# Both norms after the output projection from sums gathered per product, with all products ahead of the norms

## The chip, the cores and the metric

One core of one Trainium2 chip runs the whole program in one launch. The metric is the device time of an execution in microseconds; less is better. Engines are named as in the profile: PE is TensorE's matmul, DVE is VectorE, ACT is ScalarE, POOL is GpSimd, SP is SyncE, which issues the weight loads.

## What is computed

Two layers of one trunk over 512 latent tokens and 256 context tokens, 1024 features wide. What matters here is what stands around the output projection `w_out` of each layer, where a norm of its result `y` is added to the residual `x`, and a norm of the new `x` feeds the feed-forward part:

```python
def rmsnorm(x, g):
    y = xf * lax.rsqrt(jnp.mean(xf * xf, axis=-1, keepdims=True) + NORM_EPS)
    return y.astype(x.dtype) * g
...
    y_x = merge_heads(...) @ w_out
...
        x = x + mod_x[2] * rmsnorm(y_x, norm_mix_post[i])
        hx = modulate(rmsnorm(x, norm_ffn_pre[i]), mod_x[3], mod_x[4])
        x = x + mod_x[5] * rmsnorm(conv_ffn(hx, ...), norm_ffn_post[i])
        if not last:
            xc = xc + mod_c[2] * rmsnorm(y_c, norm_mix_post[i])
            hc = modulate(rmsnorm(xc, norm_ffn_pre[i]), mod_c[3], mod_c[4])
```

In the last layer only the latent tokens are carried on.

## The kernel before

Activations lie features first: eight tiles of 128 features by 768 tokens, columns 0 to 255 the context (`CS`), 256 to 767 the latent tokens (`XS`). Every product is made of three: `wsplit` loads 128 x 1024 weights and splits each half into a rounded `wh` (ACT, line 191) and a rest `wl` (DVE, line 192); `fsteps` then issues 24 matmuls for a tile of 128 outputs, over 8 feature tiles, of `wl` and `wh` against the activation's `hh`, `hl` (or `mh`, `ml` for the mixed heads). A product accumulates in one of **two** PSUM buffers `bb`, and the next but one can start only when ACT or DVE has read it.

The output projection (lines 375 to 395 of `layer`) runs segment by segment: `XS` then `CS` in layer 0, the two halves of `XS` in layer 1. Each segment has eight products, each copied by ACT to `y` (line 385), and then two norms. `post` makes the first: `rms` of `y` (ACT squares, line 503; sums over the tiles on DVE and POOL by turns, line 505; a sum over the partitions by matmuls with `ones`; a root and a reciprocal, lines 243 and 244; a broadcast over the partitions by matmuls, `cst,rms`; ACT copies the result to `rb`, line 521), then `y` times gate times `rb` (DVE, line 531) and `x += y` (DVE and POOL by turns, line 532). `prenorm` makes the second in the same way, from squares of the new `x`; per tile it leaves `v` (lines 543 and 547), `hh` (544, 548) and `hl` (545 on DVE, 549 and 550 with POOL), which the feed-forward products read.

Tiles come from pools with a tag and a number of buffers: squares and `v` share the tag `sq` with three buffers, sums take `acc` with four. The order of every engine's instructions is not that of the source: a scheduler, asked for by `TCK=dict(schedule_with_timeline_sim=True)`, arranges them by a timeline of its own. So products of the next part may stand ahead of norms of this one, and a change in one place can move rows in others. The same `post` and `prenorm` close the feed-forward part (`tail`), and there layer 0 hands over to layer 1: the last segment, the context, is normed while the first products of layer 1's input projection run, which ACT copies out of `bb` to `u` (line 822 of before, line 885 of the change).

Of the kernel before, what the change touches and what calls it, by code (L numbers as in the profile page):

```python
# [19 lines left out]
D = 1024  # L20
KT = 8
# [9 lines left out]
XS, CS = (256, 768), (0, 256)  # L31
# [7 lines left out]
SQB = 3  # L39
# [15 lines left out]
SQ0, MG, PR = 0, 0, 0  # L55
ACB, RBB = 4, 2
WB, RB = 3, 2
# [78 lines left out]
class Net:  # L136
# [124 lines left out]
    def main(self):  # L261
        nc, tc, a = self.nc, self.tc, self.a
# [23 lines left out]
        Np, N = self.pool("N")  # L286
# [7 lines left out]
        self.load_params(0)  # L294
        rbs = [self.rms(N, self.xt, *s, True) for s in (XS, CS)]
        self.tick(99)
# [14 lines left out]
    def layer(self, l, later):  # L311
        nc, tc, a = self.nc, self.tc, self.a
# [86 lines left out]
        g = self.gate(1)  # L399
# [89 lines left out]

    def rms(self, N, src, a, b, copy=False):  # L490

# [18 lines left out]
        for t in range(nt):  # L510
            for i, z in enumerate(acc):
                self.mm(ps[:, t:t + 1], z[:, t * 128:(t + 1) * 128], self.ones[:, 0:1], i == 0, i == len(acc) - 1)
        r = self.small(4, "rms", 4)[:, :nt]
        self.rsqrt(r, ps[:, :nt], 1.0 / D, self.eps[:, 0:1])
        ps = self.ab()
        for t in range(nt):
            self.mm(ps[:, t * 128:(t + 1) * 128], r[:, t:t + 1].to_broadcast([128, 128]), self.c("ident"), True, True)
# [4 lines left out]
        return rb  # L522

    def post(self, N, s, seg, y, g=None):
# [9 lines left out]
    def prenorm(self, N, s, seg, rb=None):  # L534

        nc, (a, b) = self.nc, seg
        sc, sh = self.coefs(s, 1 if a < 256 else 0)
        rb = self.rms(N, self.xt, a, b) if rb is None else rb
        for k in range(KT):
# [1026 lines left out]
```

## Time and profile before

| | us |
|---|---|
| median of three runs | 2274.95 (2271.13 to 2276.51) |
| the profiled execution, own time | 2278.35 |
| its span, first to last instruction | 2276.6 |
| PE busy, share of the span | 2045.0, 90% |
| DVE busy | 1310.4, 58% |
| ACT busy | 1008.7, 44% |
| POOL busy | 536.0, 24% |

Busy means that an instruction of the engine was running. PE is the engine to watch; its idle stretches, and stretches in which its granted clock is under 1.00 of full speed, are where time can be won or lost. Layer 0's output projection lies at 653 to 778 us of the span with its norms, the handover to layer 1 at 1346 to 1400 us, and layer 1's output projection at 1836 to 1932 us.

### The profile page before, as it was taken

The numbers are of one execution on the slowest core, as the hardware profiler recorded it, in microseconds if no ns is written. First come the engines' busy times: TensorE is split into PE (matmuls) and PEld (weight loads), VectorE is DVE, ScalarE is ACT, GpSimd is POOL, SyncE is SP. The second block draws the span as 40 slices with busy tenths as digits, with TensorE's granted clock in tenths as the row PEclk, the third lists the DMA queues.
The fourth block names the chain that finished last, engine by engine and source line by source line (L and its number), as shares of the span: only waits on it lengthen the run. The fifth ranks groups of instructions, "written<-read, shape, count | busy, mean of one in ns | idle before, by whom it ended". The sixth has DMA issues, their size and how long they took to land. (4 is left out here: it accounts for less than half of the span.)

```text
span 2276.6 us, 44601 instructions
## 1 busy us (share of the span) xinstructions
PE 2045.0 (90%) x18168; PEld 1672.8 (73%) x18168; DVE 1310.4 (58%) x2474; ACT 1008.7 (44%) x1928; POOL 536.0 (24%) x897
## 2 busy tenths in 40 slices
PE   7898999888888799999999969988988777999996
PEld 4677777765667578888888857876766567888886
DVE  3354535668845743354454686556667757655556
ACT  4553323565464633332232456633446446543333
POOL 1342121135502310000010143413122613211102
PEclk8799999998898999999999979999989988999997
DMA  6232345422042354422212333111412053323322
GB/s 262 67 118 100 109 148 164 143 66 68 13 149 92 121 179 167 157 103 65 66 57 66 102 109 124 61 44 62 155 43 96 6 171 102 111 94 96 99 94 92
DMA packets 85134, 235.64 MB, mean 104 GB/s; under 512 B 9088, under 2 KB 24896, under 8 KB 84928
## 3 DMA queue, kind: packets, MB, share of 16 engines
q1 hardware_dynamic: 84928, 232.78, 30.7%
q8 instruction: 143, 2.34, 0.4%
q14 instruction: 63, 0.52, 0.1%
HBM read 204.04 MB, written 28.70 MB: 102 GB/s over the span
## 5 line engine op out<-in xcount | busy, mean ns | idle before, releaser
L212 PE MATMUL bb<-hh,wl 128*128 128x512 f32 (+1 forms) x1520 | 548.3, 361 | 18.0 <-DVE wl L192 10.9
L212 PE MATMUL bb<-hl,wh 128*128 128x512 f32 (+1 forms) x1520 | 542.0, 357 | 5.8 <-POOL hl L550 4.4
L192 DVE TENSOR_TENSOR wl<-wr,wh 128x512 fp32r<-128x512 f32 (+2 forms) x452 | 338.3, 751 | 362.3 <-ACT wh L191 361.0
L212 PE MATMUL bb<-hh,wh 128*128 128x512 f32 (+1 forms) x1520 | 540.2, 355 | 0.0
L191 ACT CAST wh<-wr 128x512 fp32r<-128x512 f32 (+2 forms) x452 | 274.1, 611 | 518.0 <-PE bb L212 370.3
L212 PEld LDWEIGHTS bb<-hh,wl 128*128 128x128 f32 x1520 | 293.2, 193 | 75.2 <-DVE wl L192 14.0
L212 PEld LDWEIGHTS bb<-hl,wh 128*128 128x128 f32 x1520 | 292.8, 193 | 49.4 <-POOL hl L550 7.8
L212 PEld LDWEIGHTS bb<-hh,wh 128*128 128x128 f32 x1520 | 292.9, 193 | 39.6 <-issue 2.1
L212 PE MATMUL bb<-g,wh 128*128 128x512 f32 (+1 forms) x1024 | 263.7, 349 | 2.3 <-DVE g L192 2.3
L1441 POOL TENSOR_SCALAR y<-u,fmt 128x512 f32<-128x512 f32 (+2 forms) x88 | 80.6, 917 | 527.1 <-ACT u L824 525.6
L212 PEld LDWEIGHTS bb<-g,wh 128*128 128x128 f32 x1024 | 181.5, 195 | 27.5 <-DVE g L192 3.3
L212 PE MATMUL bb<-g,wl 128*128 128x512 f32 (+1 forms) x512 | 180.3, 354 | 21.4 <-DVE wl L192 8.5
L212 PEld LDWEIGHTS bb<-g,wl 128*128 128x128 f32 x512 | 99.2, 195 | 36.9 <-ACT g L191 9.3
L824 ACT ACTIVATE u<-bb,fmt 128x512 f32<-128x512 f32 (+1 forms) x118 | 69.0, 613 | 85.0 <-PE bb L212 85.0
L212 PE MATMUL bb<-mh,wl 128*128 128x256 f32 (+1 forms) x256 | 85.2, 333 | 23.4 <-DVE wl L192 15.5
L1468 DVE TENSOR_TENSOR y<-y,bb 128x512 f32<-128x512 f32 (+2 forms) x80 | 54.8, 686 | 82.3 <-PE bb L212 82.2
L505 POOL TENSOR_TENSOR acc<-acc,sq 128x256 f32<-128x256 f32 (+1 forms) x48 | 49.5, 1031 | 183.9 <-ACT sq L503 180.9
L1442 DVE SCALAR_TENSOR_TENSOR y<-u,fmt,y 128x512 f32<-128x512 f32 (+2 forms) x88 | 72.3, 822 | 29.6 <-POOL y L1441 29.6
L212 PE MATMUL bb<-ml,wh 128*128 128x256 f32 (+1 forms) x256 | 84.1, 329 | 0.3
L1380 ACT ACTIVATE P<-bb,ast,srq 128x768 f32<-128x768 f32 (+1 forms) x80 | 72.6, 908 | 23.4 <-DVE ast L1378 14.5
L212 PE MATMUL bb<-mh,wh 128*128 128x256 f32 (+1 forms) x256 | 82.9, 324 | 0.0
L1377 DVE TENSOR_REDUCE ast<-bb 128x1 f32<-128x768 f32 (+1 forms) x80 | 67.2, 842 | 15.9 <-PE bb L212 15.6
(519 smaller groups left out, 3680.4 us busy)
## 6 DMA issues: line engine op xcount, KB each, us to landing
wr<-in_ffn_w_in SPq DMA_DIRECT2D x92, 512.0 KB, 3.5
wr<-in_w_ada SPq DMA_DIRECT2D x80, 512.0 KB, 3.9
wr<-in_ffn_w_out SPq DMA_DIRECT2D x48, 512.0 KB, 3.5
wr<-in_w_in SPq DMA_DIRECT2D x40, 512.0 KB, 4.3
wr<-in_w_out SPq DMA_DIRECT2D x32, 512.0 KB, 3.5
aw<-in_w_ada SPq DMA_DIRECT2D x16, 512.0 KB, 8.5
x<-in_xT SPq DMA_DIRECT2D x16, 384.0 KB, 8.7
wr<-in_w_uq SPq DMA_DIRECT2D x16, 192.0 KB, 2.6
```

The costliest lines, as they stand in the source:

```text
L191: self.nc.scalar.copy(hi, src)
L192: (eng or self.nc.vector).tensor_tensor(lo, src, hi.bitcast(F32), op=ALU.subtract)
L212: self.nc.tensor.matmul(out, l, r, start=start, stop=stop)
L505: (nc.vector, nc.gpsimd)[k % 2].tensor_tensor(acc[k % 2], acc[k % 2], sq, op=ALU.add)
L824: nc.scalar.activation(u[:, a + o:b + o], ps[:, off + a:off + b], AF.Identity, bias=bias)
L1377: nc.vector.reduce_max(st[:, 0:1], sc, axis=AX)
L1380: nc.scalar.activation(P[:, :w], sc, AF.Exp, bias=st[:, 0:1], scale=self.srq[:, t:t + 1], accum_out=st[:, 1:2])
L1441: nc.gpsimd.tensor_scalar(yv, u[:, lo + 1:lo + 1 + n], cw[1], self.fm(P_FCB + i), op0=ALU.mult, op1=ALU.add)
L1442: nc.vector.scalar_tensor_tensor(yv, u[:, lo:lo + n], cw[0], yv, op0=ALU.mult, op1=ALU.add)
L1468: nc.vector.tensor_tensor(y, y, p, op=ALU.add)
```

## The change

For each product tile the new `sums` takes, from `y` as it comes, three products that are summed over the eight tiles: `y` squared (ACT), `y` times gate squared (ACT), and `y` times gate times the old `x` (DVE). With the square sum of the old `x`, which the norm before it now keeps in `ssx` (`keep=True`), the square sum of the new `x` follows once the first norm is known, and `x` is not squared again. The adds of the second sum stand on POOL, the others on DVE. `renorm` makes both norms from these sums; it is written after the products of **all** segments. The two broadcast roots stay in PSUM and are read there by DVE. Per tile DVE makes `y`, POOL adds it to `x`, DVE makes `v`, ACT `hh`, DVE `hl`. The tiles of the three products take the tag `sq` too, still with three buffers; `acc` has six in place of four.

```diff
-ACB, RBB = 4, 2
+ACB, RBB = 6, 2
...
-        for s in three if last or R3 else [XS, CS]:
+        g, done = self.gate(0), []
+        for s in three if last or R3 else [XS, CS]:
+            acc = []
             for m in range(KT):
                 wh, wl = self.wsplit(a["w_out"][l, m])
                 ps = self.bb()
                 self.fprod(ps, wh, wl, mh, ml, [s], KT, WO[l])
                 nc.scalar.copy(y[m][:, s[0]:s[1]], ps[:, 256 + s[0]:256 + s[1]])
-            self.post(Y, 0, s, y)
-            self.prenorm(Y, 1, s)
+                self.sums(Y, acc, m, y, s, g)
+            done.append((acc, s))
+        for acc, s in done:
+            self.renorm(Y, acc, y, s, g)
...
+    def sums(self, N, acc, k, y, seg, g):
...
+        for i in range(3):
+            z = N.tile([128, 512], F32, name=self.nm("z"), tag="sq" if k else "acc", bufs=SQB if k else ACB)[:, :b - a]
+            if i == 0:
+                nc.scalar.activation(z, yk, AF.Square)
+            elif i == 1:
+                nc.scalar.activation(z, yk, AF.Square, scale=gk)
+            else:
+                nc.vector.scalar_tensor_tensor(z, yk, gk, xk, op0=ALU.mult, op1=ALU.mult)
+            if k:
+                (nc.gpsimd if i == 1 else nc.vector).tensor_tensor(acc[i], acc[i], z, op=ALU.add)
...
+    def renorm(self, N, acc, y, seg, g):
...
+        rb1 = self.over(r1, nt)
...
+        rb2 = self.over(r2, nt)
+        for k in range(KT):
...
+            nc.vector.scalar_tensor_tensor(yk, yk, g[c][:, k:k + 1], rb1[:, :b - a], op0=ALU.mult, op1=ALU.mult)
+            nc.gpsimd.tensor_tensor(xk, xk, yk, op=ALU.add)
+            nc.vector.scalar_tensor_tensor(v, xk, sc[:, k:k + 1], rb2[:, :b - a], op0=ALU.mult, op1=ALU.mult)
+            nc.scalar.activation(hi, v, AF.Identity, bias=sh[:, k:k + 1])
+            nc.vector.scalar_tensor_tensor(lo, v, sh[:, k:k + 1], hi.bitcast(F32), op0=ALU.add, op1=ALU.subtract)
```

Three places show what the scheduler makes of it. Line numbers of the change are its own; numbers behind a name tell buffers of one name apart.

**DVE at the end of layer 1's output projection.** Before, the first half's `v` and `hl` stood between weight splits of the second half's products:

```order
L192 TENSOR_TENSOR wl_20046<-wr_20043,wh_20045 128x512
L192 TENSOR_TENSOR wl_20050<-wr_20043,wh_20049 128x512
L543 SCALAR_TENSOR_TENSOR v_19791<-x_19354,msc_3395_19751,rb_19789 128x256
L547 TENSOR_TENSOR v_19795<-x_19356,rb_19789 128x256
L543 SCALAR_TENSOR_TENSOR v_19800<-x_19358,msc_3395_19751,rb_19789 128x256
L192 TENSOR_TENSOR wl_20082<-wr_20079,wh_20081 128x512
L545 SCALAR_TENSOR_TENSOR hl_19384<-v_19791,msh_3396_19752,hh_19376 128x256
```

In the change they stand behind the last product's sums (`z_20160` and `z_20154` are its tiles, in the buffers that `v` takes next):

```order
L550 SCALAR_TENSOR_TENSOR z_20160<-y_19442,mg_3344_19443,x_19405 128x256
L192 TENSOR_TENSOR wl_20368<-wr_20365,wh_20367 128x512
L552 TENSOR_TENSOR z_19846<-z_19846,z_20160 128x256
L552 TENSOR_TENSOR z_19842<-z_19842,z_20154 128x256
L583 SCALAR_TENSOR_TENSOR v_20193<-x_19391,msc_3490_20163,a_20190 128x256
L583 SCALAR_TENSOR_TENSOR v_20199<-x_19393,msc_3490_20163,a_20190 128x256
L583 SCALAR_TENSOR_TENSOR v_20205<-x_19395,msc_3490_20163,a_20190 128x256
L585 SCALAR_TENSOR_TENSOR hl_19421<-v_20193,msh_3491_20164,hh_19413 128x256
```

So the `v` and `hl` of the first half moved from beneath the second half's products to after them; in layer 0 the same holds for `XS`.

**PE at the same place.** In the change the sums over the partitions of the second half stand directly behind the last product, and the first two feed-forward products are interleaved behind them:

```order
L212 MATMUL bb_20128<-mh_18440,wh_20120 128x256
L212 MATMUL b_20246<-ones,z_19842 128x1 x2
L212 MATMUL b_20246<-ones,z_19844 128x1 x2
L212 MATMUL b_20246<-ones,z_19846 128x1 x2
L212 MATMUL bb_20329<-hh_19413,wl_20333 128x256
L212 MATMUL bb_20364<-hh_19413,wl_20368 128x256
L212 MATMUL bb_20329<-hl_19421,wh_20332 128x256
```

Before, the last product was followed at once by a feed-forward product of the first half:

```order
L212 MATMUL bb_20089<-mh_18403,wl_20082 128x256
L212 MATMUL bb_20089<-ml_18411,wh_20081 128x256
L212 MATMUL bb_20089<-mh_18403,wh_20081 128x256
L212 MATMUL bb_20258<-hh_19376,wl_20262 128x256
L212 MATMUL bb_20258<-hl_19384,wh_20261 128x256
```

What moved is the first use of `hh` and `hl`: it now has the sums of the second half ahead of it.

**ACT at the handover to layer 1.** Here the context's closing norms meet the first products of layer 1 (`u<-bb` empties a product's buffer). Before:

```order
L503 ACTIVATE sq_13442<-y_7604 128x256
L822 COPY u_13621<-bb_13596 128x512
L191 CAST wh_13698<-wr_13692 128x512
L191 CAST wh_13733<-wr_13731 128x512
L822 COPY u_13674<-bb_13649 128x512
L243 ACTIVATE rms_13450<-c_13445,eps 128x2
```

In the change:

```order
L243 ACTIVATE rms_13486<-a_13481,eps 128x2
L528 COPY rb_13492<-b_13489 128x256
L509 ACTIVATE acc_13515<-x_7556 128x256
L509 ACTIVATE acc_13516<-x_7558 128x256
L509 ACTIVATE sq_13519<-x_7560 128x256
L509 ACTIVATE sq_13522<-x_7562 128x256
L509 ACTIVATE sq_13525<-x_7564 128x256
L885 COPY u_13658<-bb_13633 128x512
L509 ACTIVATE sq_13528<-x_7566 128x256
L885 COPY u_13711<-bb_13686 128x512
```

The two copies that free `bb` moved from ahead of the first norm's root to behind five squares of the second norm, though nothing in the source of this part changed but `keep=True`.

## Rows read from the trace of the kernel before

**Rows 1.** The page's first part: busy time, share of the span, instructions.

```profile
PE 2045.0 (90%) x18168; PEld 1672.8 (73%) x18168; DVE 1310.4 (58%) x2474; ACT 1008.7 (44%) x1928; POOL 536.0 (24%) x897
```

**Rows 2.** Busy time per stretch: stretch, its length, each engine, granted clock, DMA.

```profile
core 0: us, PE busy (x) PEld busy (x) DVE busy (x) ACT busy (x) POOL busy (x), PEclk, DMA share, GB/s
653.00:707.00 54.00, 52.41 (x232) 41.41 (x232) 21.38 (x31) 25.05 (x48) 3.88 (x3) 0.94 0.46 169
707.00:747.00 40.00, 29.47 (x215) 28.54 (x215) 28.88 (x36) 19.86 (x38) 11.98 (x11) 0.83 0.29 92
747.00:778.00 31.00, 20.51 (x107) 15.02 (x108) 25.96 (x39) 19.56 (x38) 16.89 (x19) 0.85 0.34 109
1836.00:1880.00 44.00, 38.26 (x278) 35.88 (x279) 26.23 (x44) 25.14 (x55) 6.13 (x7) 0.89 0.59 196
1880.00:1899.00 19.00, 18.26 (x138) 18.06 (x137) 14.19 (x29) 13.11 (x31) 4.63 (x10) 0.88 0.41 139
1899.00:1932.00 33.00, 22.00 (x152) 20.79 (x151) 24.24 (x44) 19.52 (x45) 13.01 (x16) 0.79 0.26 80
...
1370.00:1400.00 30.00, 30.00 (x146) 24.95 (x145) 24.25 (x40) 18.80 (x39) 11.88 (x14) 1.00 0.43 147
1640.00:1836.00 196.00, 151.22 (x1738) 115.78 (x1733) 135.78 (x330) 100.61 (x205) 67.35 (x99) 0.89 0.15 49
720.00:731.00 11.00, 3.93 (x18) 3.93 (x19) 10.89 (x12) 4.63 (x9) 6.59 (x5) 0.53 0.14 49
1915.00:1929.00 14.00, 6.76 (x26) 5.97 (x27) 9.20 (x19) 7.45 (x18) 4.86 (x7) 0.51 0.00 1
```

**Rows 3.** PE's waits, 653 to 778 us, then 1836 to 1937 us: total, times, longest.

```profile
PE bb L212 <- DVE wl L192: 16.6, 7, 8.5
...
PE a L212 <- DVE acc L505: 8.7, 1, 8.7
PE bb L212 <- DVE wl L192: 5.4, 3, 4.5
```

**Rows 4.** Groups by line and shape: busy us, mean ns of one, idle before.

```profile
L192 DVE TENSOR_TENSOR wl<-wr,wh 128x512 fp32r<-128x512 f32 x428 | 326.1, 764 | 358.9 <-ACT wh L191 357.8
L505 POOL TENSOR_TENSOR acc<-acc,sq 128x256 f32<-128x256 f32 x33 | 28.2, 855 | 75.3 <-ACT sq L503 72.3 <-PE bb L212 2.4
L531 DVE SCALAR_TENSOR_TENSOR y<-y,mg,rb 128x256 f32<-128x256 f32 x48 | 28.0, 652 | 1.7 <-ACT rb L521 1.7
L505 DVE TENSOR_TENSOR acc<-acc,sq 128x256 f32<-128x256 f32 x33 | 19.2, 583 | 3.6 <-ACT sq L503 3.2
L531 DVE SCALAR_TENSOR_TENSOR y<-y,mg,rb 128x512 f32<-128x512 f32 x16 | 15.0, 1008 | 0.9 <-ACT rb L521 0.9
L503 ACT ACTIVATE sq<-y 128x256 f32<-128x256 f32 x36 | 14.2, 413 | 11.8 <-DVE y L1468 8.1 <-DVE acc L505 2.8 <-POOL hl L550 0.6
L543 DVE SCALAR_TENSOR_TENSOR v<-x,msc,rb 128x512 f32<-128x512 f32 x12 | 12.8, 1068 | 0.1
L505 DVE TENSOR_TENSOR acc<-acc,sq 128x512 f32<-128x512 f32 x15 | 12.3, 819 | 8.8 <-ACT sq L503 8.6
L545 DVE SCALAR_TENSOR_TENSOR hl<-v,msh,hh 128x256 fp32r<-128x256 f32 x20 | 12.2, 611 | 1.7 <-ACT hh L544 1.5
...
L544 ACT ACTIVATE hh<-v,msh 128x512 fp32r<-128x512 f32 x12 | 8.6, 719 | 7.3 <-DVE v L543 7.3
```

**Rows 5.** Timeline at the handover: start, duration, engine, instruction, count, [idle before].

```profile
1361.45 0.56 ACT L822 COPY u<-bb 128x512 f32<-128x512 f32 x1
1362.22 1.32 PE L212 MATMUL c<-ones,acc 128*128 128x1 f32 x8 [1.24 <-DVE acc L505]
1363.40 0.48 PE L212 MATMUL bb<-hh,wl 128*128 128x512 f32 x1
...
1369.88 0.61 PE L212 MATMUL d<-cst,rms 128*128 128x128 f32 x4
1371.07 4.68 DVE L531 SCALAR_TENSOR_TENSOR y<-y,mg,rb 128x256 f32<-128x256 f32 x8
1371.45 0.39 PE L212 MATMUL bb<-hl,wh 128*128 128x512 f32 x1
1371.68 0.39 PE L212 MATMUL bb<-hh,wh 128*128 128x512 f32 x1
1376.12 0.72 ACT L503 ACTIVATE acc<-x 128x256 f32<-128x256 f32 x2 [2.64 <-DVE x L532]
```

**Rows 6.** Timeline of the second norm of layer 1's second half, 1919 to 1926 us.

```profile
1920.09 2.02 PE L212 MATMUL a<-ones,acc 128*128 128x1 f32 x8 [8.67 <-DVE acc L505]
1922.66 1.22 PE L212 MATMUL b<-cst,rms 128*128 128x128 f32 x4 [0.55 <-DVE rms L244]
1924.40 0.48 DVE L543 SCALAR_TENSOR_TENSOR v<-x,msc,rb 128x256 f32<-128x256 f32 x1 [1.79 <-ACT rb L521]
1924.92 0.51 ACT L544 ACTIVATE hh<-v,msh 128x256 fp32r<-128x256 f32 x1 [0.62 <-DVE v L543]
```

**Rows 7.** Timeline of DVE and POOL running side by side, 715 and 1345 us.

```profile
715.09 8.45 DVE L531 SCALAR_TENSOR_TENSOR y<-y,mg,rb 128x512 f32<-128x512 f32 x8 [0.28 <-ACT rb L521]
...
716.58 1.74 POOL L532 TENSOR_TENSOR x<-x,y 128x512 f32<-128x512 f32 x1 [9.84 <-DVE y L531]
...
1345.53 2.90 POOL L550 TENSOR_TENSOR hl<-v,hh 128x512 fp32r<-128x512 f32 x1 [14.82 <-ACT v L549]
1347.19 0.42 DVE L1468 TENSOR_TENSOR y<-y,bb 128x256 f32<-128x256 f32 x1
```

**Rows 8.** The tiles y at 715 to 724 us: count, ns min/median/max.

```profile
L531 DVE SCALAR_TENSOR_TENSOR y<-y,mg,rb x8: 737/749/1792, 715.1 to 721.8; 128x512 f32<-128x512 f32 x8
```

More of the change, by code (lines that the diff above doesn't have):

```diff
@@ L294, in main @@
         self.load_params(0)
-        rbs = [self.rms(N, self.xt, *s, True) for s in (XS, CS)]
+        self.ssx = self.small(6, "ssx", 2)
+        rbs = [self.rms(N, self.xt, *s, True, True) for s in (XS, CS)]
         self.tick(99)
@@ L487, in ada, with rms @@
                 yield
-    def rms(self, N, src, a, b, copy=False):
+    def rms(self, N, src, a, b, copy=False, keep=False):
         nc, n = self.nc, b - a
@@ L512, in rms @@
                 self.mm(ps[:, t:t + 1], z[:, t * 128:(t + 1) * 128], self.ones[:, 0:1], i == 0, i == len(acc) - 1)
+        if keep:
+            nc.vector.tensor_copy(self.ssx[:, a // 128:b // 128], ps[:, :nt])
         r = self.small(4, "rms", 4)[:, :nt]
         self.rsqrt(r, ps[:, :nt], 1.0 / D, self.eps[:, 0:1])
-        ps = self.ab()
-        for t in range(nt):
-            self.mm(ps[:, t * 128:(t + 1) * 128], r[:, t:t + 1].to_broadcast([128, 128]), self.c("ident"), True, True)
+        ps = self.over(r, nt)
         if PR and not copy:
@@ L522, in rms, with over @@
         return rb
+    def over(self, r, nt):
+        ps = self.ab()
+        for t in range(nt):
+            self.mm(ps[:, t * 128:(t + 1) * 128], r[:, t:t + 1].to_broadcast([128, 128]), self.c("ident"), True, True)
+        return ps
+    def sums(self, N, acc, k, y, seg, g):
+        nc, (a, b) = self.nc, seg
+        yk, xk = y[k][:, a:b], self.xt[k][:, a:b]
+        gk = g[1 if a < 256 else 0][:, k:k + 1]
+        for i in range(3):
[8 more added lines that the diff above has]
+                (nc.gpsimd if i == 1 else nc.vector).tensor_tensor(acc[i], acc[i], z, op=ALU.add)
+            else:
+                acc.append(z)
@@ new lines, in renorm @@
+    def renorm(self, N, acc, y, seg, g):
+        nc, (a, b) = self.nc, seg
+        nt, c = (b - a) // 128, 1 if a < 256 else 0
+        sc, sh = self.coefs(1, c)
+        ss = self.ssx[:, a // 128:b // 128]
+        ps = self.ab()
+        for i, z in enumerate(acc):
+            for t in range(nt):
+                self.mm(ps[:, i * nt + t:i * nt + t + 1], z[:, t * 128:(t + 1) * 128], self.ones[:, 0:1], True, True)
+        r1, r2, q = (self.small(4, n, 4)[:, :nt] for n in ("rms", "rms", "rmq"))
+        self.rsqrt(r1, ps[:, :nt], 1.0 / D, self.eps[:, 0:1])
+        rb1 = self.over(r1, nt)
+        nc.vector.tensor_tensor(q, ps[:, nt:2 * nt], r1, op=ALU.mult)
+        nc.vector.scalar_tensor_tensor(q, ps[:, 2 * nt:3 * nt], 2.0, q, op0=ALU.mult, op1=ALU.add)
+        nc.vector.tensor_tensor(q, q, r1, op=ALU.mult)
+        nc.vector.tensor_tensor(q, q, ss, op=ALU.add)
+        nc.vector.tensor_scalar(q, q, 0.0, None, op0=ALU.max)
+        self.rsqrt(r2, q, 1.0 / D, self.eps[:, 0:1])
+        rb2 = self.over(r2, nt)
+        for k in range(KT):
+            yk, xk = y[k][:, a:b], self.xt[k][:, a:b]
+            hi, lo = self.hh[k][:, a:b], self.hl[k][:, a:b]
+            v = N.tile([128, 512], F32, name=self.nm("v"), tag="sq", bufs=SQB)[:, :b - a]
+            nc.vector.scalar_tensor_tensor(yk, yk, g[c][:, k:k + 1], rb1[:, :b - a], op0=ALU.mult, op1=ALU.mult)
[3 more added lines that the diff above has]
+            nc.vector.scalar_tensor_tensor(lo, v, sh[:, k:k + 1], hi.bitcast(F32), op0=ALU.add, op1=ALU.subtract)
@@ L537, in prenorm @@
         sc, sh = self.coefs(s, 1 if a < 256 else 0)
-        rb = self.rms(N, self.xt, a, b) if rb is None else rb
+        rb = self.rms(N, self.xt, a, b, keep=True) if rb is None else rb
         for k in range(KT):
```

## The prediction

> **What bounds the kernel now.** I read the page's first part, then busy time per stretch around both output projections and the handover between the layers, then PE's waits there, and last the timeline of each wait. PE is busy for 90% of the span, DVE for 58% [rows 1]; so an instruction taken off DVE or ACT gains only where PE waits for it. The stretches show where that is [rows 2]. In layer 0, 653 to 707 us (XS products) PE is busy for 52.41 of 54.00 us: nothing to win. From 707 to 778 us (CS products, then both norms and the first feed-forward products) it is busy for 29.47 + 20.51 = 49.98 of 71 us: 21.0 us idle. In layer 1 the products from 1836 to 1899 us leave 63 − 56.5 = 6.5 us, and 1899 to 1932 us, where the second half's norms end, leaves 11.0. All PE waits of which the change could take something are in these 32 us.
>
> PE's waits name the causes [rows 3]. In layer 0 it waits 16.6 us for `wl`, once for 8.5: the weight split stands on DVE behind eight `y` of XS that take 8.45 us in a row [rows 7]. In layer 1 it waits 8.7 us for the sums of the second norm, and the clock then stands at 0.51 from 1915 to 1929 us, its lower level of 1.2 GHz, after PE had rested [rows 2, 3].
>
> **The change, layer 0's projection: −5 us.** Taken away from each segment: the second squares with their adds, and the copies `rb`. Added per product on DVE: one `y*g*x` and two adds. For 512 columns that is 1.01 + 2 x 0.82 and two weight splits of 0.76, 4.2 us [rows 4], beneath a product that takes about 54/8 = 6.7 us: free. For CS it is 0.65 + 2 x 0.58 + 2 x 0.76 = 3.35 us per product, 26.8 for eight; with the eight `y` of XS, which now come there, at 0.75 each [rows 8], some 33 us against 28.9 now, in a stretch that is 40.0 long and in which PE has 29.5 us of work [rows 2]. So DVE sets this stretch at 33 to 36 us: −4 to −7. Behind it, though, the order shows `v` and `hl` of XS behind CS's last sums, where before they ran among the products. Copy, two squares, two adds, a `v` and a `hh` make 0.4 + 0.8 + 1.2 + 1.1 + 0.7 = about 4 us of waiting, then 16 DVE instructions of some 0.95 us (15 us) [rows 4] pace two interleaved products that need about 48 x 0.23 = 11 us (the pitch of matmuls of 512 columns, 1371.45 to 1371.68 [rows 5]). That is 4 + 4 = 8 us idle, where the stretch from 747 on has 10.5 now; but CS's own norms then lie beneath feed-forward products, as the second half's do below. I take −5 for the whole of it, with ends 0 (the gain is all spent on that chain) and −11 (half of the 21 us).
>
> One term of this hangs on a detail. The eight `y` have a median of 0.75 us and a longest of 1.79 [rows 8], and the long ones lie beside POOL's adds of 1.74 us; an instruction with one operand in PSUM (L1468, 0.42 us) ran unstretched beside a POOL instruction [rows 7]. `y` and `v` now read the root from PSUM, so I take the unstretched 0.75. The Trainium skill's "SBUF — State Buffer", section "Who interferes with whom", states that as a rule: a DVE instruction with two SBUF inputs shares a locked port pair with GpSimd, and one with at most one does not; both rows agree. Were the rule not to hold for PSUM operands, the sum would be some 4 us higher in layer 0 (four adds, 1.0 each).
>
> **The handover to layer 1: +12 us.** Nothing is meant to change here, but the order does. ACT's two copies that empty layer 1's first two products from `bb` stand now behind the root of the context's first norm and five squares of its second. There are two buffers `bb`, so the third product cannot start until the first copy is done. Before, that copy ran at 1361.45 us, and the third product began at 1363.40 [rows 5]. After, the copy comes behind this chain, counted from the sums at 1362.22: sums to the first use of the root, 3.0 (4.31 from 1920.09 to 1924.40 where nothing covers it [rows 6], with PE's two parts of 2.02 and 1.22 at half clock replaced by 1.32 and 0.61 [rows 5]); first `y` to first square, 1371.07 to 1376.12 = 5.05; five squares at 0.36 = 1.8; the copy 0.56 [rows 5]. That is 10.4, so the buffer is free at 1372.6 and the product starts 9.2 us later. Can PE do other work in the meantime? From 1370 to 1400 it is busy all the time on that same row of products [rows 2], and they are queued in order behind the third. So +9, from 5 (the norm runs earlier, against the products) to 13. After a rest of 8.5 us in layer 0 PE ran at 0.53, 3.93 us of work that at full clock would have been 1.9 less; after the one in layer 1 it did 6.76 us at 0.51, 3.3 less [rows 2]. I take +3, together +12.
>
> **Layer 1's projection: −4 us.** 16 products of 256 columns now ask 16 x 3.35 = 53.6 us of DVE, and the eight `y` of the first half (5.2) lie there too: 59 us against a stretch of 63 in which PE is busy for 56.5 [rows 2, 4]. DVE and PE are level, and POOL and DVE shut each other out at times: +2. Behind the last product PE stands before the sums of the second half and needs `hh` of the first: copy, squares, adds, `v`, `hh`, 0.4 + 0.8 + 1.2 + 0.6 + 0.5 = 3.5 us [rows 4]; then 16 DVE instructions of 0.61 (9.8 us) pace two products worth 48 x 0.115 = 5.5 us: about 8 us idle in place of 11.0. With the 8.7 us rest gone, the half clock of 1915 to 1929 us (3.3) goes too, or stays short. −6, and +2: −4. Ends: −9 (no rest at all) and +3.
>
> **The rest: 0 us.** The small arithmetic on four columns, the kept square sums and the two extra `acc` tiles lie on DVE beside products; ACT has two squares per tile as before. If that cover is gone, they lie in the 3.5 us chain, at some 0.15 each. The scheduler also puts the token mixing of both layers in another order; rows cannot price that. It holds 196 − 151 = 45 us of PE idle in layer 1 [rows 2], so a tenth of it either way, ±5, is my bound, and I take 0.
>
> **Sum.** −5 + 12 − 4 = +3. The profiled execution took 2278.35 us, 3.4 above the median of the three runs; 2278.35 + 3 = 2281.4, as a median 2278.
>
> **Rivals.** (a) **Faster, 2266.** The stall at the handover does not come: the context's norm runs so early against layer 1's products that its squares are done before the second product is, and the +9 falls away with its +3, leaving 2278 − 12. For: 5 us of the chain are `y` and `x` passes that could begin sooner. Against: the order is fixed, five squares stand ahead of the copy whenever the norm runs, and PE had no gap there.
>
> (b) **Slower, 2288.** DVE becomes the bound of the products, through POOL. One add per product now runs on POOL (0.86 us for 256 columns by the adds of today [rows 4]; the 1.74 of POOL's add beside `y` [rows 7] is the longest), while DVE's `y*g*x`, adds and splits all read two SBUF operands. If each product loses 0.6 us of DVE to it, DVE needs 4.0 us per product of 256 columns. CS's eight products then lose 8 x 0.6 = 5, and layer 1's sixteen come to 64 + 5 = 69 us against 63, another 6, less the 2 already counted: +9 or 10. It decides from 3.5 us of DVE per product on, which is where 56.5 / 16 puts PE. Three `sq` buffers for squares and `v` push the same way, as a late add then holds up ACT's next square. For: the longest `y` of 1.79 us shows that such stretching is real. Against: the splits' mean of 0.76 already has some of it in it.
>
> (c) **The change doesn't do what it says, 2283.** The first segment's norms were to be hidden beneath the second's products; the order leaves only `y` there and sends `v`, `hl` behind. If these take as much on the path as the shorter product stretch gives, layer 0's −5 is 0. For: 8 us of idle are already in the sum there, where 10.5 are now. Against: the 8.5 us wait for `wl` loses its cause.
>
> **How the numbers follow.** Forecast 0.42, (a) 0.18, (b) 0.27, (c) 0.13. About 0.2%, 4.6 us, can be told from no change. Faster needs a time under 2270.4: most of (a) and a little of the forecast's lower edge, 0.19. Slower needs one over 2279.5: all of (b), most of (c) and a part of the forecast, 0.41. The same: 0.40. The range takes (a) and (b) with ±2 for the unknown order: 2266 to 2290. The forecast's own range is 2272 to 2284.
>
> **What would show it.** In the profile of the changed kernel: no 8.5 us wait for `wl` in layer 0's CS products, and 707 to 747 shortened to about 35 us; the `y` at 0.75 us or less beside POOL's adds; a PE wait of about 9 us before layer 1's third product, released by ACT's `u` copy, with a clock near 0.5 behind it; no 8.7 us wait for sums at the end of layer 1's products, but `v` or `hh` as releaser, some 8 us in many pieces. Wrong would be: no wait at the handover; waits for `wl` or `bb` among all sixteen products of layer 1 (then b); or a token mixing that is longer by more than 5 us, for which I have no row.

## The result: 1.25% slower

The changed kernel took 2302.36 us (median of four runs, 2297.33 to 2303.56) against 2273.04 us for the kernel before in the same session: a ratio of 1.0125, with a 95% interval of 1.0102 to 1.0148. The forecast was 2278, its range ended at 2290. The profiled executions differ by about as much, 2301.8 us of span against 2276.6, so the 25.2 us between them can be looked for in the traces. (The medians differ by 29.3 us. The profiled execution of before lay 5.3 us above its median, that of the change 1.2 above, so some 4 of the 29.3 us are not in these two traces.)

The first line of the page of the changed kernel, busy time and share of the span by engine, answers to [rows 1]:

```profile
PE 2072.3 (90%) x18148; PEld 1692.7 (74%) x18148; DVE 1343.5 (58%) x2554; ACT 999.4 (43%) x1904; POOL 538.5 (23%) x901
```

It says little: PE is as full as before, only of longer instructions. What helps is to lay the two traces beside each other. The products are the same, so the k-th matmul of a form in one trace answers to the k-th in the other, and the difference of their starts, as a median over those of a short window, is the delay so far. Its growth over a stretch is what the stretch lost (+) or gained (−), in us; how wide the window is taken moves a cell by up to 1.4 us. The edges of the stretches are in the time of the kernel before; the rows below the second are experiments that come later.

| kernel | start, to 100 | mixing of layer 0, to 320 | to 680 | projection and norms of layer 0, to 850 | feed-forward of layer 0, to 1310 | handover, to 1425 | mixing of layer 1, to 1855 | projection and norms of layer 1, to 1970 | feed-forward of layer 1 | sum |
|---|---|---|---|---|---|---|---|---|---|---|
| forecast | 0 | 0 | 0 | −5 | 0 | +12 | 0 | −4 | 0 | +3 |
| the change | +1.5 | +8.5 | +2.7 | −5.9 | +3.1 | +12.0 | +8.1 | −6.7 | +1.9 | +25.2 |
| e1 gate once | −2.7 | +9.1 | −1.3 | +0.1 | +1.1 | +1.4 | +3.1 | +0.3 | −0.1 | +11.0 |
| e2 six acc | +0.7 | +0.5 | −0.6 | −0.7 | 0.0 | +11.5 | +2.4 | +0.3 | −0.7 | +13.5 |
| e3 gate per segment | −3.5 | −0.9 | +1.4 | −9.2 | +4.2 | +11.8 | +4.2 | −6.6 | +2.1 | +3.4 |
| e4 keep only | −2.1 | −0.3 | −3.7 | −0.8 | +1.4 | 0.0 | −2.6 | +0.5 | −1.0 | −8.6 |
| e5 third sum in rb | −2.8 | +8.9 | −0.7 | −7.7 | +3.1 | +0.2 | +9.6 | −6.2 | +1.4 | +5.7 |
| e6 both | −2.0 | +0.1 | −5.2 | −7.3 | +3.1 | −0.1 | −0.3 | −6.1 | +2.2 | −15.6 |
| e7 both, no shift | −1.3 | −0.2 | +0.4 | −10.1 | 0.0 | 0.0 | −0.1 | −6.2 | −0.3 | −17.8 |
| e8 pad of 192 bytes | −3.1 | −0.4 | +0.9 | +2.4 | +3.1 | +4.7 | −0.9 | +0.6 | +0.4 | +7.7 |
| e9 norms in the loop | −2.9 | +2.3 | −0.1 | −14.7 | 0.0 | +4.6 | +5.4 | −10.0 | −0.2 | −15.4 |
| e10 root in SBUF | +0.6 | +2.6 | −2.6 | −2.8 | +1.1 | +1.4 | +6.8 | −0.1 | 0.0 | +6.9 |
| e11 shift of 256 | −3.6 | +0.5 | −8.9 | −7.5 | +1.2 | +1.4 | +3.2 | −6.3 | 0.0 | −20.1 |
| e12 loop in layer 1 | −1.0 | −0.4 | −5.2 | −8.6 | 0.0 | +0.2 | −2.0 | −9.9 | −0.2 | −27.1 |

How far one cell can be trusted is seen from kernels that have before's order of PE in a stretch. In the first part of layer 0's mixing (e2 to e4, e6 to e12) they lie between −0.9 and +2.6, in its second part between −8.9 and +1.4, in layer 1's mixing (e4 and e8, and e6, e7, e11 and e12, whose order differs from before's in its first third alone) between −2.6 and +3.2, and the first 100 us between −3.6 and +0.7. So a cell of 3 us is nothing in most of these stretches, and none of that second part says anything; one of 8 or 12 elsewhere that returns in several kernels is something. The sum is that of one profiled execution each and spreads likewise: e4 has −8.6 in it, and the same time as before by its runs.

What spreads there is the clock. Here are before and e11 in the second part of layer 0's mixing, cut at the same 2738 matmuls in the same order (stretch, length, then busy us of each engine, the granted clock, DMA):

```profile
320.00:650.00 330.00, 285.49 (x2738) 222.14 (x2737) 217.52 (x527) 170.52 (x341) 112.11 (x158) 0.91 0.28 89
```

```profile
316.90:639.07 322.17, 275.89 (x2738) 215.16 (x2737) 217.30 (x527) 171.24 (x341) 113.64 (x158) 0.95 0.29 91
```

PE is idle for 44.5 us in the one and 46.3 in the other. The 7.8 us between them are busy time, at a mean clock of 0.91 and of 0.95. So a loss that consists of clock alone needs more than one kernel to show it.

The two projections and the handover came out near the forecast, −12.6 and +12.0. The 25 us lie where nothing was forecast: 8.5 in the first part of layer 0's token mixing, 8.1 in layer 1's, 5.0 in the feed-forward parts, and 4.2 in the first and the third cell, too little to be told from the spread.

The stretches of the changed kernel that answer to [rows 2] (stretch, length, then busy us of each engine, the granted clock, DMA):

```profile
core 0: us, PE busy (x) PEld busy (x) DVE busy (x) ACT busy (x) POOL busy (x), PEclk, DMA share, GB/s
665.50:719.60 54.10, 51.68 (x248) 40.74 (x246) 36.82 (x50) 30.22 (x57) 10.99 (x9) 1.00 0.42 148
719.60:760.00 40.40, 31.32 (x207) 30.55 (x207) 31.15 (x49) 17.07 (x38) 17.41 (x15) 0.83 0.28 90
760.00:785.50 25.50, 22.40 (x109) 16.50 (x108) 20.93 (x44) 11.27 (x21) 9.60 (x17) 0.80 0.30 107
1866.00:1911.00 45.00, 39.21 (x285) 36.90 (x286) 38.33 (x70) 28.86 (x64) 12.41 (x15) 0.92 0.58 193
1911.00:1930.60 19.60, 17.68 (x120) 16.87 (x119) 16.11 (x27) 10.65 (x25) 5.63 (x11) 0.85 0.46 137
1930.60:1957.00 26.40, 21.48 (x158) 20.54 (x159) 24.54 (x60) 13.81 (x31) 7.72 (x9) 0.94 0.32 102
```

The first three are layer 0's XS products, CS products, and norms with the first feed-forward products. CS's products took 40.4 us, before 40.0: no gain there. The gain is behind them, 25.5 us in place of 31.0. In layer 1 the products took 64.6 us in place of 63.0, the norms 26.4 in place of 33.0, and the clock in them stood at 0.94 in place of 0.79.

### The profile page after: what moved, and what is told of

Its sections match the earlier page's. It is cut to its first block, busy times and chain, and to the rows that moved or that the text cites. A ratio compares the mean times of both kernels' runs of the same rounds, so it can differ in the third digit from the quotient of the medians.

```text
span 2301.8 us, 44678 instructions
## 1 busy us (share of the span) xinstructions
PE 2072.3 (90%) x18148; PEld 1692.7 (74%) x18148; DVE 1343.5 (58%) x2554; ACT 999.4 (43%) x1904; POOL 538.5 (23%) x901
## 5 line engine op out<-in xcount | busy, mean ns | idle before, releaser
L212 PEld LDWEIGHTS bb<-hh,wh 128*128 128x128 f32 x1520 | 295.0, 194 | 40.4 <-issue 2.3
L1505 DVE SCALAR_TENSOR_TENSOR y<-u,fmt,y 128x512 f32<-128x512 f32 (+2 forms) x88 | 71.9, 817 | 37.1 <-POOL y L1504 37.1
L1506 DVE SCALAR_TENSOR_TENSOR y<-u,fmt,y 128x512 f32<-128x512 f32 (+2 forms) x88 | 72.6, 825 | 2.5
```

What stands on the lines that cost most here:

```text
L212: self.nc.tensor.matmul(out, l, r, start=start, stop=stop)
L1505: nc.vector.scalar_tensor_tensor(yv, u[:, lo:lo + n], cw[0], yv, op0=ALU.mult, op1=ALU.add)
L1506: nc.vector.scalar_tensor_tensor(yv, u[:, lo + 2:lo + 2 + n], cw[2], yv, op0=ALU.mult, op1=ALU.add)
```

## The experiments

Theory: what the change lost outside the projections it lost by side effects of three lines that have nothing to do with the sums, namely an order of instructions, a buffer's address, and a shift of addresses. Rival: the sums' own work loses it, by DVE and POOL instructions that hold up others.

### e1: the gate alone

```diff
+        g = self.gate(0)
         for s in three if last or R3 else [XS, CS]:
...
-            self.post(Y, 0, s, y)
+            self.post(Y, 0, s, y, g)
```

> The kernel before, with one edit: the gate of the output projection (four DVE instructions on 8 columns) is made once per layer ahead of its products, as in the change, and not once per segment. No sums, both norms as before. The order of PE differs from before in layer 0's token mixing in the same places as the change's, and in a part of layer 1's mixing; the handover between the layers and both output projections keep their order. Theory O (the loss of the change outside the projections is the order of the scheduler): layer 0's mixing, 150 to 300 us, loses 8 to 12 us as in the change; layer 1's mixing 0 to 9; total +8 to +20. Theory S (the loss comes from the work of the sums): within 2 us of before everywhere.

Measured: 2291.93 us, ratio 1.0079 (1.0062 to 1.0096), with +9.1 us in the first part of layer 0's mixing, where the change lost 8.5. Before, `post` of each segment made a gate of its own, four instructions of DVE on 128 x 8 each; the change makes one for both segments. The scheduler places these small instructions early, into the mixing: in before the eight of layer 0 run at 160.5 to 162.8 us. With four fewer of them its timeline moves a little there, and from there on it sorts PE, DVE and ACT differently. PE's waits in that stretch, the change first, then e1 (engine, tile, line, released by; us in total, times, longest):

```profile
PE c L212 <- DVE r L994: 3.8, 1, 3.8
PE a L212 <- ACT part L489: 2.5, 1, 2.5
```

```profile
PE c L212 <- DVE r L932: 4.8, 1, 4.8
PE a L212 <- ACT part L484: 2.5, 1, 2.5
```

The same two waits stand in both, though e1 has no sums; before had none over 1.3 us there. The stretches, before (150 to 300 us) and e1:

```profile
150.00:300.00 150.00, 140.36 (x3138) 111.13 (x3136) 77.78 (x200) 52.04 (x114) 32.98 (x31) 0.97 0.33 110
```

```profile
147.30:306.50 159.20, 146.85 (x3147) 116.39 (x3145) 77.47 (x197) 55.56 (x117) 33.41 (x32) 0.94 0.32 104
```

Only 2.7 of the 9.2 us are idle time of PE (159.20 − 146.85 against 150.00 − 140.36). The other 6.5 are busy time for nearly the same matmuls, at a mean granted clock of 0.94 in place of 0.97. The mean is made of two levels, 1.00 and 0.50 (2.4 and 1.2 GHz): by the clock's records in the traces it stood at 0.50 for 18.3 us in e1 and for 9.4 before, and PE worked for 16.9 and 7.4 us of these. As a matmul takes about twice as long there (0.42 us to the next in place of 0.23, as the part on the prediction shows), that makes an estimated (16.9 − 7.4) / 2 = 4.8 us; what the remaining 1.7 are is not told apart. PE waits less often in e1, 6 times for over 0.3 us against 12, but longer, up to 4.8 us against 1.3, and in or just behind each of its waits of 4.8, 2.5 and 1.7 us the clock was at 0.50. So here a reorder cost more than its waits show. The rival falls for this part: the loss is there with no sums.

### e2: six buffers for sums, nothing else

```diff
-ACB, RBB = 4, 2
+ACB, RBB = 6, 2
```

> The kernel before, with one edit: ACB 6 in place of 4, so six buffers for the sums of a norm; nothing else. The order is the same up to the handover; there ACT's two copies of layer 1's first products stand behind five squares of the context's second norm, as in the change, and PE's order differs in part of layer 1's mixing. Theory O: +12 us at the handover (the third product of layer 1 waits about 9 us for a PSUM buffer, with a clock near 0.5 behind it), 0 to +9 in the mixing of layer 1, nothing elsewhere: +12 to +21. Theory S: more buffers can only take waits away: 0 or a small gain.

Measured: 2288.45 us, ratio 1.0062 (1.0046 to 1.0077), with +11.5 us at the handover and nothing up to there. PE's longest wait of the handover, in the change and in e2:

```profile
PE bb L212 <- ACT u L885: 7.9, 1, 7.9
```

```profile
PE bb L212 <- ACT u L822: 7.9, 1, 7.9
```

ACT's rows of the change, answering to [rows 5] (start, duration, instruction, count, idle before): the copies to `u` stand between the squares of `x`.

```profile
1381.77 0.72 ACT L509 ACTIVATE acc<-x 128x256 f32<-128x256 f32 x2 [5.06 <-DVE x L595]
1382.70 1.03 ACT L509 ACTIVATE sq<-x 128x256 f32<-128x256 f32 x3 [0.20 <-DVE x L595]
1383.63 0.56 ACT L885 COPY u<-bb 128x512 f32<-128x512 f32 x1
```

More buffers made a kernel slower that had no use for them. The addresses in the program say how. The pool of the norms lies below the tiles `y`. With `acc` at four buffers `y` ends at byte 150,944 of a partition, and layer 1's `u` begins at 151,392. Two more buffers of 2 KB push `y` up to 155,040 in e2 and 155,232 in the change: the last tiles of `y` now lie where `u` will be. A copy into `u` must then wait until the context's last `y` has been added to `x`. The change's trace has this wait: POOL writes the edges of `u` ahead of the copy, and it could not do so before DVE's last add of `y` to `x`,

```profile
1383.42 0.10 POOL L879 MEMSET u<- 128x2 f32 x1 [1.10 <-DVE x L595]
```

0.2 us before the copy starts. The order of ACT, which the prediction took for the cause, then only follows that wait.

### e5: the third sum in tiles that lie idle

The change, with `acc` at four buffers again; the third sum of each segment takes the two buffers of `rb`, which `renorm` doesn't need.

```diff
-ACB, RBB = 6, 2
+ACB, RBB = 4, 2
...
-... tag="sq" if k else "acc", bufs=SQB if k else ACB)[:, :b - a]
+... tag="sq" if k else ("acc", "acc", "rb")[i], bufs=SQB if k else (ACB, ACB, RBB)[i])[:, :b - a]
```

> The change, with one edit: the third sum of each segment takes the tag rb, which the new norms leave unused, and ACB is 4 again. So the pool is as large as before and the tiles y no longer reach into the addresses (from byte 151392 of each partition) where layer 1's u lies. Theory M (the handover's stall comes from that overlap: a copy into u must wait until the last y there has been read): the 8 us wait goes, some 12 us less than the change, 2288 to 2293; layer 0's mixing still loses its 9 us. Theory T (it comes from the scheduler's timeline, which the sums shift in time): the stall stays, 2300 to 2304.

Measured: 2289.19 us, ratio 1.0065 (1.004 to 1.0089), and +0.2 at the handover. PE's longest wait there is back to before's (1.2 us for the sums):

```profile
PE a L212 <- DVE acc L511: 1.2, 1, 1.2
```

The sums are in this kernel, in full, so theory T falls: the stall came from the 4 KB.

### e3: the change with a gate per segment

```diff
-        g, done = self.gate(0), []
+        done = []
         for s in three if last or R3 else [XS, CS]:
-            acc = []
+            acc, g = [], self.gate(0)
```

> The change, with one edit: the gate is made once per segment, as before, so four small DVE instructions more. The order of PE in layer 0's mixing is then word for word that of before; the handover and layer 1's mixing differ still. Theory O: the 9 to 12 us that layer 0's mixing lost come back, the handover's +12 stays, layer 1's mixing is between 0 and +9: 2280 to 2292. Theory S: no gain against the change, 2302.

Measured: 2283.42 us, ratio 1.0037 (1.0022 to 1.0052), 19 us less than the change, with −0.9 in the first part of layer 0's mixing in place of +8.5. The handover's +11.8 stays, as it should; layer 1's mixing has +4.2 in place of +8.1.

### e4: the kept sums alone

```diff
+        if keep:
+            nc.vector.tensor_copy(self.ssx[:, a // 128:b // 128], ps[:, :nt])
```

> The kernel before, with the kept square sums of the first two norms alone: two DVE copies of 4 and 2 columns at the start, nothing else; the order is that of before on PE throughout. Theory O: same as before within 2 us, among it perhaps the 1.5 us that the change loses at 35 to 45 us. Theory S says the same. It is the measure of what a run of the same order gives: if the matmul pitch in the feed-forward part comes out at 0.5% more, as in the change's profile, that is no matter of the change.

Measured: 2276.58 us, ratio 1.0006 (0.9995 to 1.0016): the same. The start came out at −2.1, so the change's +1.5 there is no effect of it. But the feed-forward of layer 0 lost 1.4 us, with the same instructions in the same order (that of layer 1 gained 1.0). That is the third side effect.

### e6, e7, e8, e11: both edits, and a shift of addresses

In the change `ssx` and `rmq` take 192 bytes ahead of the tiles for weights and for `hh`, `hl`, and move all of these; in e4 it is 64. e6 is the change with the edits of e3 and e5, still shifted by 192. e7 is e6 with the new small sums put into bytes that were there already, so nothing is shifted. e8 is the kernel before with an unused tile of 192 bytes. e11 is e6 with 64 bytes more, a shift of 256.

```diff
-        self.eps = S.tile([128, 2], F32, name="eps")
+        self.eps = S.tile([128, 8], F32, name="eps")
...
-        self.ssx = self.small(6, "ssx", 2)
+        self.ssx = self.eps[:, 2:8]
...
-... for n in ("rms", "rms", "rmq"))
+... for n in ("rms", "rms", "rms"))
```

```diff
+        nc.gpsimd.memset(self.small(48, "pad"), 0.0)
```

> The change with both edits, the gate per segment and the third sum in rb. The order of layer 0's mixing, of the handover and nearly all of layer 1's mixing is then that of before. If the losses are additive: the projections' gains remain (13 to 15 us), against them 4 to 5 us of longer matmul pitch in both feed-forward parts: 2264 to 2270, faster than before. If the sums themselves cost something elsewhere: 2272 to 2280.

> As the last, and the kept sums lie in spare columns of the tile eps, the temporary q in the tag rms: no tile of the weights or of hh moves by the 192 bytes that they moved in the change. Theory A (the feed-forward's longer matmul pitch in the change, 0.5%, comes from the addresses of the tiles): the pitch is that of before, 4 to 5 us less than with the shift, 2259 to 2266. Theory N (it is the chip or the execution): no difference.

> The kernel before with one unused tile of 192 bytes ahead of the weights' tiles; the same instructions in the same order. Theory A: +2.8 us over layer 0's feed-forward part and +1.8 over layer 1's, as the change's profile has, so 2278 to 2281. Theory N: 2273 to 2277, the pitch as before.

> The kernel of e6 (both edits, tiles shifted by 192 bytes) with one more unused tile of 64 bytes ahead, so that the weights' tiles are shifted by 256 bytes. Theory A1 (any shift lengthens the pitch by the place of tiles against each other, as those of layer stages that are allocated from the other end don't move): pitch 229 ns and more, 2263 to 2268 as e6. Theory A2 (what counts is the shift modulo 256 bytes): pitch 228.3 ns as before and e7, 2259 to 2264.

Measured: e6 2265.20 us, ratio 0.9958 (0.994 to 0.9976); e7 2261.76, 0.994 (0.9916 to 0.9964); e8 2283.41, 1.0037 (1.0016 to 1.0057); e11 2258.39, 0.9944 (0.9928 to 0.996). e8 came out above and e11 just below what was expected. The medians of e6, e7 and e11 lie too near each other to be told apart, but a stretch tells it. The same 1826 matmuls of layer 0's feed-forward (one more at the edge in e7), with the clock at 1.00 and PE never idle, in before, the change, e8, e7 and e11:

```profile
900.00:1200.00 300.00, 300.00 (x1826) 259.96 (x1825) 136.04 (x178) 90.95 (x164) 26.53 (x92) 1.00 0.27 92
```

```profile
906.94:1208.87 301.93, 301.93 (x1826) 261.20 (x1825) 135.91 (x178) 90.40 (x163) 26.52 (x92) 1.00 0.27 91
```

```profile
900.05:1201.98 301.93, 301.93 (x1826) 261.18 (x1825) 136.23 (x178) 91.33 (x164) 26.66 (x92) 1.00 0.27 91
```

```profile
888.79:1188.80 300.01, 300.01 (x1827) 259.96 (x1826) 136.14 (x178) 90.78 (x164) 26.59 (x92) 1.00 0.27 92
```

```profile
880.43:1180.43 300.00, 300.00 (x1826) 259.98 (x1825) 136.19 (x178) 90.63 (x163) 26.71 (x92) 1.00 0.28 92
```

With 192 bytes of shift they take 301.93 us, with none or 256 they take 300.00. The same stretch took 301.93 in e6 and 301.11 in e4, with 64 bytes; of the other kernels, those with 192 bytes (e3, e5) have the longer time too, and those with none (e1, e2, e9, e10, e12) the shorter. So the pitch of the matmuls, from the start of one to the start of the next, depends on where their tiles lie, and a shift by 256 bytes leaves it as it was. The traces also say which matmuls: the time with matmuls that read `g` running (the feed-forward's inner activation), before and e8, then that with those that read `hh` (stretch, length, busy us and count, clock, DMA):

```profile
900.00:1200.00 300.00, 87.36 (x502) 1.00 0.27 92
900.05:1201.98 301.93, 89.28 (x502) 1.00 0.27 91
```

```profile
900.00:1200.00 300.00, 190.41 (x763) 1.00 0.27 92
900.05:1201.98 301.93, 190.36 (x763) 1.00 0.27 91
```

All 1.9 us are in the products that read `g`. Its tiles are allocated from the other end and stay where they were, while their weights moved by 192 bytes. The products of `hh` and `hl`, whose weights moved by as much and the activations with them, kept their pace. So what counts is not the place of the weights alone; it goes with the place of weights and activation against each other. Why, the runs don't show. In the change the feed-forward parts lost 5.0 us together; e8, which has the shift alone, has +3.1 and +0.4 of them, so the shift is most of it.

e8 lost 4.7 us at the handover too, where e6 with the same shift lost none. The stretch in before and in e8, at the same 472 matmuls:

```profile
1310.00:1425.00 115.00, 95.06 (x472) 79.14 (x472) 84.53 (x130) 69.24 (x126) 48.40 (x48) 0.88 0.34 113
```

```profile
1312.90:1432.60 119.70, 99.95 (x472) 82.78 (x471) 84.69 (x130) 69.91 (x127) 49.36 (x48) 0.84 0.32 109
```

PE is idle for 19.9 and 19.8 us: no wait was added, the clock was lower. Why it was lower there stays open.

The sum of e6 is as its expectation had it: the losses of the change were additive, and taking two of them away left a kernel that is faster than before. With this the rival falls for the whole: e7 has the sums in full, and no stretch of it lost more than 0.4 us. The loss in layer 1's mixing went with them: −0.3 in e6 and −0.1 in e7, where the change had +8.1 and e5 +9.6. It is shown less well than that of layer 0. e1 and e2, with one edit each, have +3.1 and +2.4 there, within the spread, and of the 7.9 us that the change's trace loses between 1425 and 1855 us of before only 1.8 are idle time of PE, the rest busy time at a clock of 0.90 in place of 0.92. That the order is its cause is likely, since e10, whose order moved there as well, has +6.8; it is not shown.

### e9 and e12: where the norms are written

e9 is e7 with `renorm` inside the loop, after the products of its own segment; e12 has it there in layer 1 alone.

```diff
-            done.append((acc, s, g))
-        for acc, s, g in done:
             self.renorm(Y, acc, y, s, g)
```

> The kernel of e7 (the change with the gate per segment, the third sum in rb, nothing shifted), with one edit: renorm stands inside the loop, after the products of its own segment, not after those of all segments. The sums stay. Theory P (what the projections gain comes from the sums; where the norms are written matters little, as v and hl wait for sq buffers anyway): within 3 us of e7 in each projection, 2259 to 2266. Theory Q (it is the place behind all products that gains, since the first segment's norms then don't stand among the second's weight splits on DVE): a wait of 5 to 9 us for wl in layer 0's CS products, 2266 to 2274.

> The kernel of e7 with renorm inside the loop in layer 1 alone, after the products of each half; layer 0 as in e7. The order is e7's up to layer 1's output projection, so the handover and layer 1's mixing keep their time. From e9 layer 1's projection should gain 4 us more than in e7, layer 0's stays: 2255 to 2260. If the place of the norms makes no difference there (the gain seen in e9 then came from how its mixing ended): 2260 to 2264 as e7.

Measured: e9 2255.29 us, ratio 0.9933 (0.9913 to 0.9953); e12 2254.54, 0.9931 (0.9907 to 0.9954). Neither theory had this: the norms in the loop gain more than behind all products, −14.7 in place of −10.1 in layer 0 and −10.0 in place of −6.2 in layer 1. PE does wait for `wl` in e9's projection of layer 0, though seven times for 4.4 us at most, not once for 5 to 9 as theory Q said,

```profile
PE bb L212 <- DVE wl L192: 11.4, 7, 4.4
```

and over the whole stretch (650 to 850 us of before) PE is idle as long as in e7, 22.4 us against 22.3; what e9 gains more there is clock, 0.94 in place of 0.92. Kernels with e7's order in that stretch (e6, e7, e11, e12) lie between −7.3 and −10.1. In layer 1 (1828 to 1970 us of before) PE's idle time is 18.7 us in e9 and 18.6 in e12 against 20.1 in e7; the rest is busy time, at a clock of 0.94 and 0.92 against 0.90. So "all products ahead of the norms" was no gain in itself; what gains is the sums together with the root that is read in PSUM (see e10). e9 loses 10 us in the handover and layer 1's mixing. The 4.6 at the handover come with e7's order there and, as in e8, with 19.8 us of idle time and a clock of 0.84; in the mixing its order moved again. e12 keeps e7's order in both. Whether e12 is faster than e7 as a whole the intervals don't tell; its −9.9 in layer 1's projection, the same as in e9, says that this part is.

### e10: the root in SBUF

```diff
-        rb1 = self.over(r1, nt)
+        rb1 = N.tile([128, 512], F32, name=self.nm("rb"), tag="rb", bufs=RBB)
+        nc.scalar.copy(rb1[:, :b - a], self.over(r1, nt)[:, :b - a])
```

> The kernel of e7, with one edit: ACT copies the first norm's broadcast root from PSUM to rb, and DVE's y reads it there, so y has two operands in SBUF again. Theory L (y is stretched beside POOL's adds because both of its operands lie in SBUF): some of the y of 512 columns take 1.7 us again in layer 0, where e7 and the change have 0.75 for all; +2 to +5 us in layer 0's projection. Theory K (the stretch has another cause): y stays at 0.75. The order of layer 1's mixing moves in this kernel, so its total says little: 2262 to 2280.

Measured: 2280.28 us, ratio 1.0025 (1.0009 to 1.0041). The tiles `y` in layer 0 (count; shortest, median, longest in ns), in the change and in e10 (16 there, eight of them of 256 columns), answering to [rows 8]:

```profile
L581 DVE SCALAR_TENSOR_TENSOR y<-y,mg,d x8: 734/736/748, 730.9 to 737.7; 128x512 f32<-128x512 f32 x8
```

```profile
L582 DVE SCALAR_TENSOR_TENSOR y<-y,mg,rb x16: 487/614/1758, 720.1 to 765.9; 128x512 f32<-128x512 f32 x8, 128x256 f32<-128x256 f32 x8
```

and POOL's adds beside the change's `y`:

```profile
L582 POOL TENSOR_TENSOR x<-x,y x6: 1262/1510/1728, 732.8 to 740.5; 128x512 f32<-128x512 f32 x6
```

With the root in PSUM not one of eight `y` was stretched, and seven of them ran while POOL did; with it in SBUF the longest is 1.76 us again, as before's 1.79. The eight of XS now take 10.9 us in a row,

```profile
720.12 10.88 DVE L582 SCALAR_TENSOR_TENSOR y<-y,mg,rb 128x512 f32<-128x512 f32 x8
```

and behind them PE waits 10.6 us for `wl`, where its longest such wait is 4.9 in e7. It costs more than the 2 to 5 us expected: layer 0's projection gains 2.8 us, where e6, e7, e11 and e12 gain 7.3 to 10.1, and layer 1's nothing in place of 6.2. A part of that is the ACT copy's and the moved order's, and isn't told apart. But e10 has the sums in full, and with them alone the projections gain little. So a large part of what the new norms gain seems to hang on the root in PSUM; with the order moved too, that is not shown. The section "Who interferes with whom" of the Trainium skill's page "SBUF — State Buffer" was drawn on for the forecast; the trace agrees with it for DVE operands in PSUM.

## Why the prediction was wrong, point by point

**The handover was right, in place and size, though not in its cause.** Forecast +12: a chain of 10.4 us from the sums to the free buffer, and +3 for the clock. Measured +12.0: the sums began at 1373.63 us and the copy ended at 1384.19, 10.6 us; PE waited 7.95, and then ran its first matmuls at half pace:

```profile
1373.63 0.35 PE L212 MATMUL a<-ones,acc 128*128 128x1 f32 x2 [0.33 <-DVE acc L511]
...
1384.25 0.79 PE L212 MATMUL bb<-hh,wl 128*128 128x512 f32 x1 [7.95 <-ACT u L885]
...
1385.27 0.63 PE L212 MATMUL bb<-hh,wh 128*128 128x512 f32 x1
1385.69 0.63 PE L212 MATMUL bb<-hh,wl 128*128 128x512 f32 x1
```

0.42 us from one to the next where [rows 5] have 0.23. Over the stretch that answers to 1310 to 1425 us of before, shown under e8,

```profile
1321.20:1448.20 127.00, 98.78 (x472) 82.00 (x471) 84.44 (x132) 71.81 (x128) 49.18 (x52) 0.85 0.31 101
```

PE's idle time grew by 8.3 us (28.2 against 19.9) and its busy time by 3.7, where 9 and 3 were forecast. But the reason given, that the order changed and only `keep=True` stood in this part's source, was not the cause; the buffer count was, by way of the address. `ACB` is a number for every norm, and it stands in the diff's first line.

**The projections were right in sum, in layer 0 by luck.** Forecast −9, measured −12.6. In layer 1 both halves of the term hold: products +1.6 (forecast +2), what is behind them −6.6 (−6). In layer 0 the size held, −5.9 (−5), but not the place, and two errors of about 5 us cancelled: CS's products took 40.4 us, not 33 to 36. The 8.5 us wait for `wl` became shorter ones, 7.7 us in three:

```profile
PE bb L212 <- DVE wl L192: 7.7, 3, 4.9
PE bb L212 <- ACT y L388: 2.2, 1, 2.2
```

and the gain came behind, where 8 us of waiting were forecast and 3.1 were left (25.50 − 22.40): CS's norms lie beneath feed-forward products more fully than the estimate had it.

Rival (b) is seen in layer 0. While POOL adds the eight `y` of XS to `x`, DVE's rows with two operands in SBUF take up to three times as long as without,

```profile
738.84 6.25 POOL L582 TENSOR_TENSOR x<-x,y 128x512 f32<-128x512 f32 x4
```

```profile
738.40 2.71 DVE L192 TENSOR_TENSOR wl<-wr,wh 128x512 fp32r<-128x512 f32 x2
742.46 1.51 DVE L550 SCALAR_TENSOR_TENSOR z<-y,mg,x 128x256 f32<-128x256 f32 x1
...
757.78 0.48 DVE L550 SCALAR_TENSOR_TENSOR z<-y,mg,x 128x256 f32<-128x256 f32 x1 [0.55 <-ACT y L388]
758.23 0.69 DVE L192 TENSOR_TENSOR wl<-wr,wh 128x512 fp32r<-128x512 f32 x1
```

and PE's wait of 4.9 us ends at 739.49, when the first of these two `wl` is there, behind an add of 1.41 us and four `y`. How much of the 5 us of CS's products this stretching makes is not told apart. The forecast counted the unstretched 0.75 of `y`, rightly, and means for the rest. In layer 1 rival (b) is not seen: the products took 1.6 us more, not 6.

**The step that failed is "The rest: 0 us".** It set the reordered token mixing at nothing, with ±5 us as a bound "a tenth of it either way" of PE's idle time in layer 1. Two things were wrong in it. The bound was taken from layer 1 alone, and layer 0's mixing, reordered as widely, got no term; its first part lost 8.5 us. And idle time is no measure for what a reorder can cost: in e1 6.5 of 9.2 us are not waits but longer busy time, an estimated 4.8 of it by a lower clock. Layer 1 lost 8.1, beyond the bound. The shifted tiles, most of the 5.0 us over both feed-forward parts, had no term at all; no row of before could have priced them. A mixing that is longer by more than 5 us stands among the prediction's own signs of being wrong, and it came.

**Why the range did not hold.** It ended 12 us above the forecast and took the slower side from one mechanism in the projections. The reordered stretches and the shifted tiles all came out as losses, and the range had ±2 for them. With 8.5 + 8.1 + 5.0 for them the sum would have come to 25 in place of 3.

## What to carry to other kernels

- Before costing what an edit does, list what it touches besides: how many instructions a scheduler is handed, how large a pool is and which tiles come to lie on others, and by how many bytes tiles behind it move. Here these parts of the kernel lost 8.5 + 12.0 + 8.1 + 5.0 = 33.6 us, more than twice what the new norms gained in the projections (12.6).
- Where a scheduler sets the order, compare the order of the whole program first, and mend the edit until it is unchanged wherever the edit has no business; only then measure. Mended so, the same idea went from 1.25% slower to 0.6% faster.
- Before explaining a difference between two stretches, split it into PE's idle time and its busy time, and look at the granted clock: with one order, the delay over a stretch differed by up to 10 us between kernels here, and the clock differed with it.
- An operand that DVE read from PSUM saved a copy on ACT, and DVE was not stretched beside POOL.

## What the runs showed of the hardware

- The same 1826 matmuls, with PE never idle and the clock at 1.00, took 300.00, 301.11 and 301.93 us with their tiles shifted by 0, 64 and 192 bytes in each partition, and 300.00 with 256. With 192 the whole difference lies in matmuls whose weights moved and whose other operand did not (87.36 to 89.28 us); where both had moved, there is none (190.41 and 190.36).
- A reorder that gave PE fewer but longer waits in layer 0's mixing (up to 4.8 us in place of 1.3) went with a mean clock of 0.94 in place of 0.97, and cost 2.7 us of idle time and 6.5 of busy time.
- The same 2738 matmuls in the same order, with 44.5 and 46.3 us of idle time, took 330.00 us at a mean clock of 0.91 and 322.17 at 0.95.
- DVE's 512-column product with one operand in PSUM took 0.73 to 0.75 us eight times of eight, seven of them beside POOL's instructions; with both in SBUF it took up to 1.76. Two weight splits of 512 columns took 2.71 us together beside POOL's adds, where one alone took 0.69.
